# Hybrid attention layer on one core: a pacing ratio of its own for the latent projection between the chunked score tiles

## The chip, the core and the metric

The kernel runs on one core of a Trainium2 chip. A core has five engines with a queue each, which work in order: TensorE (PE in the profile; PEld is its loading of weights, which overlaps the matmuls), VectorE (DVE), ScalarE (ACT), GpSimd (POOL) and SyncE (SP), which here issues the transfers. The metric is the device time of one execution in microseconds (us). An engine's busy time is the sum of its instructions' durations.

## The reference

One layer of a streaming encoder on x of 1024 rows by 1024 columns, float32:

- an adaptive normalisation: six rows of shift, scale and gate from a conditioning vector times `w_ada`;
- one input projection of the normalised rows, whose columns are a query latent (256), a key and value latent (128), a rotary key (32), and queries, keys and values of eight chunked heads of 64;
- latent attention: the latents are normalised, projected up to eight heads (96 wide for queries and keys, 64 for values), normalised per head, rotated, and attend to all earlier chunks of 64 rows;
- chunked attention: eight heads, each chunk of 64 queries sees its own and the eight chunks before it, with a relative bias;
- an output projection with a gated residual, then a gated feed-forward part with a causal convolution of width 3, and a second gated residual.

```
q = rmsnorm(q_lat) @ w_q_up          # latent heads
kv = rmsnorm(kv_lat) @ w_kv_up
...
o_mla = mla_attention(q, k, v)       # 8 heads, chunk-causal
o_ca = chunk_attention(cq, ck, cv, rel_bias)   # 8 heads, band of 9 chunks
x = x + g_a * (concat(o_mla, o_ca) @ w_out)
```

## The kernel before

**Stages.** After a start in which the rows are normalised and transposed into `hT`, one long attention stage runs (in the profile some 540 us), then the output projection, the feed-forward part and the down projection. Matrix products are made with three matmuls each, since every operand is kept as a high and a low half (`gemm3`, lines 150 to 157).

**Score tiles.** The attention stage is a list of units: sixteen for the chunked heads, written here as chunked unit (p, g, o) with the pair of heads p, the half of the query rows g and the head o of the pair, then sixteen for the latent heads. Each unit has four tiles of 128 queries, so that tile 7 of unit (3, 1, 1) is the last chunked one. A tile (`scores`, lines 774 to 866) makes its scores on TensorE (`sc` for the chunked heads, `sm` for the latent ones), takes the minimum on DVE, the exponential on ACT, scales on POOL and DVE into two half-precision parts (`hlc`, `hlm`) and has a transposing transfer turn them (`PTc`, `PTm`). Three tiles later `values` (lines 868 to 906) multiplies the turned tiles of a pair with the values (`pvc`, `pvm`), and writes a finished half of a head to memory (`oc`, `om`, then `oT_d`).

**Fillers.** Between the tiles stand steps of the projections that are needed later, in a fixed order (lines 963 and 964): the remaining chunked projections, then "m", the latent projection (`f_m`, lines 502 to 536), "up0" and "up1", the two latent up projections (`f_up`, lines 628 to 691), and "oca", half of the output projection. "m" has 38 steps: for each of eight row tiles four steps of six matmuls into `mp`, after every fourth tile three steps that turn the latents into a page of `latT` (transposes into `lt_ps`). A row tile's matmuls are followed by its normalisation on ACT and POOL (`lat`). An up projection has 16 steps, two for each row tile, `qu` and `ku`; a tile's results go through ACT and POOL, and through eleven instructions of DVE, into `qn`, `kn` and `vt`. Before its first step it loads its weights `wq` and `wk` through two buffers that `f_m` also uses (`qtile`, line 141), splits them into halves on ACT and POOL, and makes a scale (`vspm`).

**Pace.** `pace` (lines 1005 to 1012) is called after the scores of every tile and after every `values`, with a written cost in nanoseconds of what was just issued. It adds that cost times a ratio to a debt and issues filler steps, which bring their own written cost, until the debt is paid. The ratio is `R_CA` = 1.9 for a chunked unit and `R_MLA` = 0.5 for a latent one. `need` (lines 996 to 1001) issues at one go whatever a unit must have and isn't issued yet: the first latent unit needs all of "up0", the second (the upper half of the same head) all of "up1". Every 1700 ns of written cost of most fillers, "m" among them, also issue a step of `f_ada` (lines 436 to 479), which loads and sums the remaining rows of the adaptive normalisation.

**What sets an engine's order.** The order in which the program issues is not yet the order of a queue. The framework orders each engine's queue while the kernel is built: of the instructions that are ready it takes the one with the lowest position, which is the place in the program; a block under `high_priority(offset=n)` counts as if it stood n places earlier. Scores and their softmax stand 400 places earlier (`OFF_S`), the scaling and the transfer 200 (`OFF_P`), the values 200 (`OFF_V`); fillers, and the pages that a unit prepares, stand at their own place. A filler step must also stay behind the fifth-last block of scores or values issued before it (`gemm3_f`, `LAG`).

Of the kernel before, what the change touches and what calls it, by code (L numbers as in the profile page):

```python
# [43 lines left out]
MODE_C = "1111"  # L44
MODE_M = "1111"
PSCALE, VSCALE = 2.0 ** 15, 2.0 ** 14
R_CA, R_MLA = 1.9, 0.5


C_C, C_GA, C_GM, C_B, C_GQL, C_GKL = 0, 8, 16, 24, 72, 74  # L50
# [14 lines left out]
def layer_kernel(ctx, tc, I, out):  # L65
# [331 lines left out]
    def f_qk(p):  # L397
        with tc.issue_after(r_last):
            w, _ = weights(f"qk{p}")
        for h in range(2):  # L400
            qns[p, h] = pgtile([P, 4, 256], F32, f"qn{p}_{h}")
        for t in range(0, NT, 2):
            pt = ps.tile([P, 512], F32, name=f"ipq{p}_{t}", tag="mm", bufs=2)
            yield from proj2(pt, t, w, 256)
            qk_norm(pt[:], f"{p}_{t}", qns[p, t // 4], t % 4)

    def f_v(pp):
        w, ssw = weights(f"v{pp}") if pp else (wv0, ssw0)
        for t in range(0, NT, 2):
            h, j = divmod(t, 4)  # L410
            if t == 0:
                for i in range(2):
                    vts[2 * pp + i] = apg.tile([P, NT, 2, 2, 64], F16, name=f"v{2 * pp + i}", tag="v16", bufs=3)
            pt = ps.tile([P, 512], F32, name=f"ipv{pp}_{t}", tag="mm", bufs=2)
            yield from proj2(pt, t, w, 256)
            if t == 0:
                vscale["c", pp] = pow2_scale(f"c{pp}", ssw[:], hb[:], ND, 2.0 * D)
                sc = vscale["c", pp][0]
            for i in range(2):
                vt = vts[2 * pp + i][:, t:t + 2]  # L420
                src = pt[:].rearrange("p (t q a b) -> p t q a b", t=2, q=2, a=2)[:, :, i]
                act.activation(vt[:, :, :, 0, :], src, AF.Copy, scale=sc)
                dve.scalar_tensor_tensor(vt[:, :, :, 1, :], src, sc, vt[:, :, :, 0, :], op0=MUL, op1=SUB)
# [282 lines left out]
    def f_oca():  # L706
        ws = [load_wo(4, n, "a", "p") for n in range(2)]
        for t in range(NT):
            lo = rtile(f"cl{t}", (P, 4, P), F32R)
            hi = rtile(f"ch{t}", (P, 4, P), F32R)  # L710
            sp.dma_start(f32(lo[:]), oT_d[4:8, :, t * P:(t + 1) * P].rearrange("k p t -> p k t"))
            hi_of("a", hi[:], f32(lo[:]))
            lo_of("p", lo[:], f32(lo[:]), hi[:])
            for n in range(2):
                pt = ps.tile([P, 512], F32, name=f"oc{t}_{n}", tag="mm", bufs=2)
                yield from gemm3_f(pt[:], [(hi[:, k], lo[:, k], ws[n][k][:, 0], ws[n][k][:, 1]) for k in range(4)])
                o = qtile(f"co{t}_{n}")
                act.activation(o[:], pt[:], AF.Copy)
                sp.dma_start(part_d[t][:, n * 512:(n + 1) * 512], o[:])
# [227 lines left out]
    def mla_unit(gr, hh, g):  # L947
        o = hh % 2

        def prep():  # L950
# [12 lines left out]
    fillers = [("v0", f_v(0)), ("qk1", f_qk(1)), ("qk2", f_qk(2)), ("v1", f_v(1)), ("qk3", f_qk(3)),  # L963
               ("m", f_m()), ("up0", f_up(0)), ("up1", f_up(1)), ("oca", f_oca())]
# [5 lines left out]
    def fill_step():  # L970
        while fillers:
            key, gen = fillers[0]
            try:
                c = next(gen)
            except StopIteration:
                done.add(key)
                fillers.pop(0)
                continue
            if key in ("qk1", "qk2", "v1", "qk3"):
                nstep[0] += 1  # L980
                if nstep[0] % 3 == 0:
                    one_ahead(fillers[1][0])
            if key == "qk1":
                if rope[0] is None:
                    rope[0] = rope_tables()
                with tc.issue_after(anchor["dve"]):
                    next(rope[0], None)
            if key not in ("v0", "up0", "up1", "oca"):
                nside[0] += c
                while nside[0] > 1700:  # L990
                    nside[0] -= 1700
                    next(side[0], None)
            return c
        return None
# [8 lines left out]
    debt = [0.0]  # L1003

    def pace(cost, ratio):
        debt[0] += cost * ratio
        while debt[0] > 0:
            c = fill_step()
            if c is None:
                debt[0] = 0.0  # L1010
                return
            debt[0] -= c
# [9 lines left out]
    for n in range(len(tiles) + DEPTH):  # L1022
        if n < len(tiles):
            u, i = tiles[n]
            if i % 4 == 0 and u not in ready:
                need(u.need)
                u.prep()
            if i % 4 == 2 and n + 2 < len(tiles):
                v = tiles[n + 2][0]
                if all(k in done for k in v.need):  # L1030
                    ready.append(v)
                    v.prep()
            pace(u.scores(i), R_CA if u.band else R_MLA)
        if n >= DEPTH:
            u, i = tiles[n - DEPTH]
            if i % 4 == 1:
                need(u.needv)
            if i % 2:
                pace(u.values(i), R_CA if u.band else R_MLA)
# [609 lines left out]
```

## Time and profile before

| what | us |
|---|---|
| median of three runs (1331.05 to 1333.88) | 1333.68 |
| the profiled execution, as timed | 1334.5 |
| its span from first to last instruction | 1332.7 |
| TensorE busy / its loading of weights | 1212.8 / 997.1 |
| DVE busy | 1088.7 |
| ACT busy | 622.3 |
| POOL busy | 572.3 |
| first and last matmul of the latent projection start at | 264.1 / 335.9 |
| last chunked score matmul starts at | 325.6 |
| first matmul of the first up projection starts at | 348.0 |
| first latent score matmul starts at | 374.7 |
| last latent score matmul starts at | 595.3 |

Rows of a view of groups give line, engine, operation and names, then minimum, median and longest duration in ns, or the busy time and the mean. A row of the timeline gives the start, the time that a merged run of equal instructions took, and, in brackets, for how long the engine had been idle before it and what ended that. A row of the view by windows gives, for a stretch of the span, its length and then busy time and count of PE, PEld, DVE, ACT and POOL, the granted TensorE clock as a share of full speed, and what the DMA engines did. A busy time of TensorE counts overlapping matmuls once, so that distances between starts tell more of its pace than single durations do.

### The profile page before, as it was taken

How to read it: one execution, taken by the hardware profiler on the slowest of the kernel's cores; microseconds unless marked ns; L12 is line 12 of the kernel's file. 1: busy time of each engine (PE TensorE's matmuls, PEld its weight loads, DVE VectorE, ACT ScalarE, POOL GpSimd, SP SyncE). 2: the span in 40 equal slices, each digit the busy share in tenths (PEclk: the TensorE clock that was granted, in tenths of full speed). 3: DMA queues.
4: the chain of work that ended last, by engine and by line, in shares of the span. 5: the costliest groups of instructions: out<-in, count | busy, mean ns of one | idle time of the engine just before them, and what ended most of it. 6: DMA issues, size and time to landing. Idle time of an engine off the chain costs nothing.

```text
span 1332.7 us, 18710 instructions
## 1 busy us (share of the span) xinstructions
PE 1212.8 (91%) x6168; PEld 997.1 (75%) x6168; DVE 1088.7 (82%) x1928; ACT 622.3 (47%) x1132; POOL 572.3 (43%) x610
## 2 busy tenths in 40 slices
PE   3899999989667798888889999999999998999998
PEld 3888878868555576666677888888888886888886
DVE  6979898877589967894779888898889986687667
ACT  5454654445555545553366444444443444443331
POOL 5476773675675633354615445444444541000000
PEclk9899999989878798997999999999999998999999
DMA  8416768766123685879702333333333336943441
GB/s 321 144 55 156 164 143 197 150 151 138 35 72 70 119 172 122 152 164 326 275 16 79 106 124 111 122 116 108 113 106 132 111 119 221 393 151 114 132 159 63
DMA packets 223689, 190.57 MB, mean 143 GB/s; under 512 B 148708, under 2 KB 166884, under 8 KB 223592
## 3 DMA queue, kind: packets, MB, share of 16 engines
q1 hardware_dynamic: 223592, 189.38, 50.3%
q8 instruction: 48, 0.79, 0.3%
q14 instruction: 49, 0.40, 0.1%
HBM read 117.24 MB, written 37.49 MB: 116 GB/s over the span
## 4 chain that ended last, share of the span: by engine, by line
PE 48%; DVE 3%; DMA 2%; issue 1%; ACT 1%; POOL 0%; SPq 0%; POOLq 0%; DVEq 0%
PE p L1125 10%; PE p L1126 10%; PE p L1127 10%; PE dnA_P L1460 2%; PE dnA_P L1461 2%; PE dnA_P L1462 2%; PE dnB_P L1461 1%; PE dnB_P L1460 1%; PE dnB_P L1462 1%; PE dnA L1461 1%; PE dnA L1460 1%; PE dnA L1462 1%; PE dnB L1461 1%; PE dnB L1462 1%; PE dnB L1460 1%
## 5 line engine op out<-in xcount | busy, mean ns | idle before, releaser
L77 ACT ACTIVATE dnP<-dnr 128x1024 fp32r<-128x1024 f32 x73 | 77.4, 1064 | 117.5 <-PE dnA_P L1462 46.4
L1434 DVE TENSOR_TENSOR dnP<-dnr,dnP 128x1024 fp32r<-128x1024 f32 x72 | 87.9, 1224 | 52.7 <-ACT dnP L77 47.7
L73 POOL TENSOR_SCALAR hlm<-Pm,rim 128x512 f16<-128x512 f32 (+2 forms) x96 | 65.4, 691 | 77.5 <-DVE rim L832 32.0
L84 POOL TENSOR_TENSOR wf<-wu,wf 128x512 fp32r<-128x512 f32 x22 | 39.8, 1808 | 118.2 <-ACT wf L77 118.2
L1296 DVE SCALAR_TENSOR_TENSOR u<-c,cvp,u 128x1023 f32<-128x1023 f32 x44 | 58.6, 1372 | 27.8 <-ACT u L1295 27.8
L84 POOL TENSOR_TENSOR wb<-wu,wb 128x512 fp32r<-128x512 f32 x22 | 42.2, 1920 | 75.0 <-ACT wb L77 59.6
L73 POOL TENSOR_SCALAR hlc<-Pc,ric 128x640 f16<-128x640 f32 (+2 forms) x64 | 48.0, 753 | 54.5 <-DVE ric L832 25.8
L851 DVE SCALAR_TENSOR_TENSOR hlm<-Pm,rim,hlm 128x512 f16<-128x512 f32 (+2 forms) x96 | 65.9, 696 | 5.5 <-POOL hlm L73 5.2
L829 ACT ACTIVATE Pc<-sc,mc 128x640 f32<-128x640 f32 (+2 forms) x64 | 42.2, 660 | 55.2 <-DVE mc L818 26.1
L891 PE MATMUL pvm<-PTm,vt 128*128 128x256 f16 (+1 forms) x320 | 47.7, 302 | 22.1 <-DMA PTm<-hlm 14.2
L829 ACT ACTIVATE Pm<-sm,mm 128x128 f32<-128x128 f32 (+3 forms) x64 | 47.1, 738 | 37.7 <-DVE mm L822 21.2
L1295 ACT ACTIVATE u<-c,cvp 128x1024 f32<-128x1024 f32 x44 | 52.4, 1238 | 26.0 <-DVE c L1394 18.0
L1297 DVE SCALAR_TENSOR_TENSOR u<-c,cvp,u 128x1022 f32<-128x1022 f32 x44 | 61.7, 1442 | 0.0
L891 PEld LDWEIGHTS <-vt 128*128 128x128 f16 x320 | 33.1, 111 | 37.0 <-issue 21.6
L77 ACT ACTIVATE wc<-ws 128x512 fp32r<-128x512 f32 x21 | 13.3, 632 | 91.9 <-DVE ws L1144 86.1
L154 PE MATMUL ipq<-wq_s,hT 128*128 128x256 f32 x192 | 55.7, 290 | 0.0
L156 PE MATMUL ipq<-wq_s,hT 128*128 128x256 f32 x192 | 55.4, 288 | 0.0
L155 PE MATMUL ipq<-wq_s,hT 128*128 128x256 f32 x192 | 55.1, 287 | 0.0
L851 DVE SCALAR_TENSOR_TENSOR hlc<-Pc,ric,hlc 128x640 f16<-128x640 f32 (+2 forms) x64 | 49.2, 774 | 6.8 <-POOL hlc L73 6.7
L1461 PE MATMUL dnA_P<-dnP 128*128 128x512 f32 x132 | 51.3, 389 | 0.0
L1462 PE MATMUL dnA_P<-dnP 128*128 128x512 f32 x132 | 51.3, 389 | 0.0
L1460 PE MATMUL dnA_P<-dnP 128*128 128x512 f32 x132 | 51.2, 389 | 0.0
(442 smaller groups left out, 4413.7 us busy)
## 6 DMA issues: line engine op xcount, KB each, us to landing
wu<-w_up SPq DMA_DIRECT2D x44, 512.0 KB, 3.5
dnr<-g_d SPq DMA_DIRECT2D x73, 256.0 KB, 2.8
aw<-w_ada SPq DMA_DIRECT2D x48, 256.0 KB, 3.4
g_d<-u SPq DMA_DIRECT2D x22, 512.0 KB, 3.0
dnr<-w_down SPq DMA_DIRECT2D x44, 256.0 KB, 5.4
adaw<-w_ada_a SPq DMA_DIRECT2D x16, 512.0 KB, 6.0
x<-x SPq DMA_DIRECT2D x16, 512.0 KB, 9.8
g_d<-gs SPq DMA_DIRECT2D x22, 256.0 KB, 2.8
```

The costliest lines, as they stand in the source:

```text
L73: pool.tensor_scalar(o, i, s, 1.0, op0=MUL, op1=MUL)
L77: act.activation(o, i, AF.Copy)
L84: (pool if eng == "p" else dve).tensor_tensor(o, i, f32(hi), op=SUB)
L829: act.activation(pr[:, :n], sv, AF.Exp, bias=m[:], scale=-1.0, accum_out=rsum[:, 0:1])
L851: dve.scalar_tensor_tensor(hl[:, w:2 * w], pp, ri[:], hl[:, :w], op0=MUL, op1=SUB)
L1125: pe.matmul(pt, sh, pg[:, 0], start=(k == 0 and not add), stop=False, skip_group_check=skip)
L1126: pe.matmul(pt, sh, pg[:, 1], start=False, stop=False, skip_group_check=skip)
L1127: last = pe.matmul(pt, sl, pg[:, 0], start=False, stop=(k == 3), skip_group_check=skip)
L1434: r = f(*a, **k)
L1460: pe.matmul(pt, sh, w[:, 0, 0], start=start, stop=False, skip_group_check=add)
L1461: pe.matmul(pt, sh, w[:, 1, 0], start=False, stop=False, skip_group_check=add)
L1462: pe.matmul(pt, sl, w[:, 0, 0], start=False, stop=stop, skip_group_check=add)
```

## The change

While the filler in front of the list is "m", the latent projection, `pace` replaces the ratio that it was given by `R_M` = 3.2. Nothing else is edited: no instruction is added or removed, and the values computed are the same. What changes is after which tile the steps of "m", of all fillers behind it, and of `f_ada`, are issued.

```
-R_CA, R_MLA = 1.9, 0.5
+R_CA, R_M, R_MLA = 1.9, 3.2, 0.5
...
     def pace(cost, ratio):
+        if fillers and fillers[0][0] == "m":
+            ratio = R_M
         debt[0] += cost * ratio
         while debt[0] > 0:
             c = fill_step()
```

More of the change, by code (lines that the diff above doesn't have):

```diff
@@ L46 @@
 PSCALE, VSCALE = 2.0 ** 15, 2.0 ** 14
-R_CA, R_MLA = 1.9, 0.5
+R_CA, R_M, R_MLA = 1.9, 3.2, 0.5
 C_C, C_GA, C_GM, C_B, C_GQL, C_GKL = 0, 8, 16, 24, 72, 74
@@ L1005, in pace @@
     def pace(cost, ratio):
+        if fillers and fillers[0][0] == "m":
+            ratio = R_M
         debt[0] += cost * ratio
```

## The prediction, made before the changed kernel had run

> **What bounds the kernel now.** I read the page first, then a view by windows around the place where the change acts (chunked heads end, latent heads begin), then the timelines of the engines there.
>
> ```profile
> span 1332.7 us, 18710 instructions
> ...
> PE 1212.8 (91%) x6168; PEld 997.1 (75%) x6168; DVE 1088.7 (82%) x1928; ACT 622.3 (47%) x1132; POOL 572.3 (43%) x610
> ```
>
> Over the whole span no engine is full, so the bound has to be found for each stretch:
>
> ```profile
> 298.00:312.00 14.00, 14.00 (x79) 12.72 (x78) 11.68 (x31) 6.99 (x23) 11.20 (x24) 1.00 0.83 188
> 312.00:326.00 14.00, 13.34 (x85) 10.38 (x83) 10.58 (x34) 5.93 (x13) 3.08 (x4) 1.00 0.61 122
> 326.00:336.00 10.00, 9.72 (x53) 9.43 (x53) 5.62 (x12) 5.93 (x25) 8.98 (x21) 1.00 0.41 80
> 336.00:348.00 12.00, 5.87 (x40) 4.41 (x39) 2.32 (x4) 5.67 (x16) 8.30 (x22) 0.70 0.38 94
> 348.00:375.00 27.00, 19.81 (x83) 14.62 (x83) 22.02 (x75) 16.52 (x39) 12.94 (x14) 0.94 0.03 8
> 375.00:460.00 85.00, 60.74 (x272) 45.91 (x272) 77.03 (x232) 46.82 (x112) 54.72 (x58) 0.78 0.41 89
> ```
>
> The reader is to see three stages. Up to 336 TensorE has no gap worth naming (14.00 of 14, 13.34 of 14, 9.72 of 10): the chunked heads and the latent projection are bound by it. From 348 DVE sets the pace (22.02 of 27, then 77.03 of 85). Between them lies a hole of 12 us in which TensorE is busy for 5.87 and DVE for 2.32, and the clock falls to 0.70. The order around the hole stands in TensorE's timeline and in the windows of `mp` alone:
>
> ```profile
> 320.63 1.16 PE L891 MATMUL pvc<-PTc,v 128*128 128x256 f16 x11
> ...
> 323.83 1.27 PE L891 MATMUL pvc<-PTc,v 128*128 128x256 f16 x12 [0.24 <-DMA PTc<-hlc]
> 324.91 0.59 PE L797 MATMUL sc<-k,qh 128*128 128x128 f32 x2
> 325.43 0.60 PE L797 MATMUL sc<-k,ql 64*128 64x128 f32 x2
> ```
>
> ```profile
> 312.00:326.00 14.00, 5.04 (x24) 4.35 (x24) 0.00 (x0) 1.00 0.61 122
> 326.00:336.00 10.00, 9.10 (x48) 8.91 (x48) 1.45 (x3) 1.00 0.41 80
> ```
>
> ```profile
> 335.86 0.35 PE L156 MATMUL mp<-wm_h,hT 128*128 128x416 f32 x1
> ...
> 338.96 0.33 PE L530 MATMUL lt_ps<-ident,lat 128*128 128x128 f32 x1 [1.43 <-POOL lat L522]
> 339.42 1.27 PE L891 MATMUL pvc<-PTc,v 128*128 128x256 f16 x12
> 342.12 0.47 PE L530 MATMUL lt_ps<-ident,lat 128*128 128x128 f32 x1 [1.43 <-POOL lat L522]
> 344.16 1.11 PE L530 MATMUL lt_ps<-ident,lat 128*128 128x128 f32 x4 [1.56 <-DVE latT L534]
> 346.84 1.11 PE L530 MATMUL lt_ps<-ident,lat 128*128 128x128 f32 x4 [1.57 <-DVE latT L534]
> 348.04 0.67 PE L154 MATMUL qu<-wq,latT 128*128 128x384 f32 x1
> ```
>
> The last chunked scores start at 324.91. Behind them 48 of the 192 matmuls of "m" (eight of its 32 matmul steps) run as one block, with no scores left to stand beside. After the block TensorE waits 1.43 + 1.43 + 1.56 + 1.57 = 6.0 us in four pieces, and "up0" starts at 348.04, 12.0 us after the last `mp` at about 336.05. That delay is a chain, which the other queues show:
>
> ```profile
> 337.39 1.12 SPq L637 DMA_DIRECT2D wqr<-w_qu  x2
> ...
> 343.40 0.33 SPq L643 DMA_DIRECT2D wkr<-w_kvu  x1
> ```
>
> ```profile
> 340.30 0.52 ACT L77 ACTIVATE wq<-wqr 128x384 fp32r<-128x384 f32 x1 [2.49 <-DMA wqr<-w_qu]
> ```
>
> ```profile
> 342.05 0.37 POOL L523 TENSOR_SCALAR lat<-lat,mr 128x128 f32<-128x128 f32 x1
> 342.38 1.95 POOL L84 TENSOR_TENSOR wq<-wqr,wq 128x384 fp32r<-128x384 f32 x2
> ```
>
> The loads of `wq` wait for the two buffers that the last row tiles of "m" use, their split waits on POOL behind the last `lat`, the load of `wk` (343.40) waits for the first split to free a buffer, and `vspm` and `qu` follow. It starts from the end of "m", wherever that lies.
>
> **The change part by part.** *Where the steps are issued* follows from the written costs. At 1.9 the 38 steps of "m" reach from tile 5 of unit (2,1,1) to the values issued just before the last chunked tile; "up0" gets four steps beside the tiles and twelve at one go in `need`. At 3.2 "m" ends with the values issued before tile 5 of (3,1,0), all 16 steps of "up0" follow by tile 6 of (3,1,1), `need` has none of it left, and the go of "up1" before the second latent unit falls from eight steps to four.
>
> *What the queues make of it* I count by places: a score tile some 15 instructions, a block of values 14, a step of "m" six and its share of the normalisation. Before, the last score tile, 400 places forward, outranks the later steps of "m", as the 48 matmuls behind it show. After, the last step of "m" stands about 30 places ahead of the last score tile even with its 400. Up to tile 6 of (3,1,0) the count gives the order that the trace already has, because until then the scores, not the steps, wait for their inputs. So only the last four score tiles move: 4, 5, 7 and 11 more steps of "m" ahead of them.
>
> *The end of "m".* What it overtakes no longer stands in front of it: the last score tile, 324.91 to 326.03 or 1.1 us, and two blocks of values, 1.16 + 1.27 us. Together 3.5 us, so "m" ends at about 332.6. Bounds: 0 if the order stays; if nothing but `mp` ran from 312 on, its 72 matmuls left there (24 + 48; 48 take 9.10 us, so 13.7) would end at 325.7, 10 us early, which the higher places of the earlier scores exclude. I take 3.5.
>
> *The start of "up0".* The overtaken 3.5 us fit into the 6.0 us of gaps in the hole. The chain keeps its 12.0 us, except that its splits on POOL now have the last tiles' work beside them. A split beside a busy DVE and one in the hole:
>
> ```profile
> L84 POOL TENSOR_TENSOR wm_l<-wm_r,wm_h 128x256 fp32r<-128x256 f32 x4 | 3.8, 950 | 3.7 <-ACT wm_h L77 3.6
> ```
>
> ```profile
> L84 POOL TENSOR_TENSOR wq<-wqr,wq 128x384 fp32r<-128x384 f32 x2 | 1.9, 994 | 0.0
> ```
>
> 950 ns for 256 columns against 994 for 384 (663 for 256) is 1.43 times as long. On two `wq` splits (1.95 us, 0.84 more) the price lies between 0 and 0.8; with about 6 us of moved tile work on DVE in 12 us, and a POOL scaling or two between, I take 0.7. "up0" starts 3.5 - 0.7 = 2.8 us earlier.
>
> The Trainium skill ("SBUF — State Buffer", "Who interferes with whom") speaks against the change here: VectorE and GpSimd share one port pair as an exclusive lock, and a two-input VectorE instruction keeps a reading GpSimd instruction out until it is done. By it a split that comes second waits whole scalings; the slower split above agrees with the direction.
>
> *The clock.* After the hole TensorE starts slowly:
>
> ```profile
> 351.23 0.34 PE L154 MATMUL qu<-wq,latT 128*128 128x384 f32 x1
> ...
> 353.55 0.34 PE L154 MATMUL qu<-wq,latT 128*128 128x384 f32 x1
> ```
>
> The first row tile's nine matmuls take 3.2 us (348.04 to 351.23), the second's 2.3 (to 353.55). A hole with 2.5 instead of 6.0 us of gaps may keep the clock up: 0 to 0.9 us, I take 0.5.
>
> *From 348 on* "up1" has five more steps ahead of the first latent unit's pages. In 348 to 375 DVE idles 18%, in 375 to 460, where latent tiles and "up1" mix, 9%. Mixed as well, 22.02 us of DVE would take 24.3: a gain of 2.7 at best. At worst a page waits for DVE with "up1" ahead of it, as here, 2.4 us:
>
> ```profile
> 383.42 0.45 PE L729 MATMUL mq_ps<-ident,qn 128*96 128x128 f32 x1 [2.37 <-DVE qn L500]
> ```
>
> Between +2.4 and -2.7 I take -0.7, since the work that moves up is what DVE lacks there.
>
> *`f_ada`.* Its calls and transfers stay, the remaining ones come up to a few tiles sooner, on SP ahead of some `PTc`:
>
> ```profile
> L460 DVE SCALAR_TENSOR_TENSOR aacc<-aw,cs,aacc 128x512 f32<-128x512 f32 x9 | 7.5, 830 | 0.1
> ```
>
> ```profile
> PE pvc L891 <- DMA PTc<-hlc: 1.9, 2, 1.6
> ```
>
> DVE has 5.7 us free in 298 to 326 and hides sums of 0.83 that slip by a tile; without that cover each would cost its 0.83 once. A late transfer has cost up to 1.6 us at one place. I take 0, with 1.6 as the upper end.
>
> **Sum:** -2.8 - 0.5 - 0.7 = -4.0 us. Against the profiled execution that is a span of 1328.7 and a time of 1330.5; its 1334.5 stands 0.8 over the median of 1333.68, so I predict 1329.7. What lies behind 605 us doesn't change in itself and is carried along.
>
> **Rivals.** *The tail of the chunked heads holds up "up0"* (slower). The last score tile now starts near 333 or 334. From there to the last values it takes 14.5 us before (324.91 to 339.42), some of it in POOL's queue:
>
> ```profile
> 334.88 1.09 DVE L851 SCALAR_TENSOR_TENSOR hlc<-Pc,ric,hlc 128x640 f16<-128x640 f32 x1 [3.95 <-POOL hlc L73]
> ```
>
> So the last `pvc` is due at 348 to 352 (3.95 us of waiting behind `lat` may come twice). If it still stands ahead of `qu` in TensorE's queue, as it does before by 8.6 us, "up0" waits for it plus 1.3 us and starts at 349.3 to 353.3. It decides from a last transfer that lands later than about 346.7. Price +1.3 to +5.3, middle 3.3: 1337.0. For it: the queue is in order and POOL is busy 8.30 of 12 in the hole. Against: by place `qu` comes before the last two blocks of values.
>
> *The order doesn't change.* If readiness, and not places, decides, the 48 matmuls stay behind the last score: 1333.7. For it: up to 312 the trace goes by readiness. Against: from 320 the steps of "m" are ready and yet let two blocks of values and the last tile pass.
>
> *The splits lose to DVE.* If each of the chain's three splits waits out one scaling like the 1.09 us above, they cost 3.3 instead of 0.7: the sum is -1.4, 1332.3. For it: the split of 950 ns. Against: 3.3 us of such scalings is all that the moved tiles have in the hole. The rule of the Trainium skill ("SBUF — State Buffer") cited above leads here.
>
> *The hole closes.* If the tail also keeps TensorE filled, all 6.0 us of gaps go, with the clock's 0.9 and the 2.7 of mixing: -9.6, 1324.1. For it: the moved work is of the right size. Against: the chain from the end of "m" is untouched.
>
> **How the numbers follow.** Forecast 0.40, tail 0.24, no change 0.16, splits 0.06, hole closed 0.14. About 0.2% or 2.7 us is what a measurement of this kernel tells from no change. The forecast's own range, from the bounds of the clock, the mixing and the transfers, is 1326 to 1333; three quarters of it lie over 2.7 us. Faster: 0.31 of the forecast's 0.40, the 0.14, and 0.02 of no change, 0.47. Slower: 0.20 of the tail's 0.24, 0.03 of no change (the queues after 460 are ordered anew as well) and 0.05 of the forecast by the upper ends of mixing and transfers: 0.28. The rest, 0.25, is the same. For 8 in 10 the range takes in the closed hole, a little beyond it, and the tail to its upper end: 1322 to 1339.
>
> **What would show it.** Right: no block of `mp` behind the last `sc`; `mp` ends near 332 or 333; `sc` ends after it; `qu` starts near 345; the windows before 312 as they are. Wrong: `qu` starts at 348 or later with a `pvc` just ahead of it that waited for `PTc` (tail); 40 or more `mp` behind the last `sc` (no change); a start of `qu` before 343 (hole closed). If the first up projection is earlier and the time is not, the gain went between 348 and 605, and the latent scores' first and last start tell where.

## The result and the profile after

The changed kernel took 1352.22 us (median of four runs, 1348.96 to 1354.44) against 1333.76 beside it: a ratio of 1.0137 with a 95% interval of 1.0109 to 1.0165. It is 18 us slower, outside the range that was given. The profiled execution has the span of the first line here; the second is the page's line of busy times.

```profile
span 1352.7 us, 18718 instructions
...
PE 1222.1 (90%) x6168; PEld 1004.3 (74%) x6168; DVE 1095.3 (81%) x1928; ACT 623.0 (46%) x1132; POOL 582.8 (43%) x610
```

The same instructions are done in 20 us more. The view by windows of the kernel after, for the stretches shown of before (length, then busy time and count of PE, PEld, DVE, ACT, POOL, then clock, DMA share, GB/s):

```profile
298.00:312.00 14.00, 14.00 (x78) 12.87 (x77) 7.15 (x15) 4.42 (x17) 11.19 (x24) 0.95 0.65 174
312.00:326.00 14.00, 11.30 (x69) 10.57 (x68) 3.34 (x6) 5.33 (x19) 3.09 (x13) 1.00 0.15 37
326.00:336.00 10.00, 8.07 (x47) 7.67 (x45) 1.88 (x3) 5.32 (x20) 8.12 (x24) 1.00 0.07 20
336.00:348.00 12.00, 10.56 (x32) 7.55 (x33) 9.57 (x27) 5.40 (x12) 7.43 (x11) 0.54 0.41 92
348.00:375.00 27.00, 20.15 (x97) 14.28 (x95) 23.86 (x80) 14.24 (x35) 13.74 (x15) 0.83 0.41 79
375.00:460.00 85.00, 57.56 (x281) 44.51 (x282) 78.05 (x228) 50.08 (x118) 55.57 (x54) 0.84 0.32 75
```

DVE's column tells the story. From 298 to 336 DVE did 27.9 us of work before; now it does 12.4. TensorE, full before, has 4.6 us of idle time there. The work turns up from 336 on, where the latent heads need DVE for themselves. What went missing in 298 to 336 are the last eight chunked score tiles, as TensorE's timeline of the kernel after shows:

```profile
301.76 0.47 PE L797 MATMUL sc<-k,qh 128*128 128x512 f32 x1
302.16 0.50 PE L797 MATMUL sc<-k,ql 64*128 64x512 f32 x1
307.85 0.38 PE L530 MATMUL lt_ps<-ident,lat 128*128 128x128 f32 x2
...
322.47 0.66 PE L530 MATMUL lt_ps<-ident,lat 128*128 128x128 f32 x4 [1.57 <-DVE latT L534]
327.92 0.60 PE L729 MATMUL q_ps<-ident,qn 128*128 128x128 f32 x4
333.06 0.57 PE L797 MATMUL sc<-k,qh 128*128 128x512 f32 x2
333.48 0.60 PE L729 MATMUL k_ps<-ident,qn 128*128 128x128 f32 x4
336.29 0.33 PE L797 MATMUL sc<-k,qh 128*128 128x128 f32 x1 [2.22 <-DVE k L762]
```

Between 302 and 333 there is no chunked score. The rows to look at are `q_ps` and `k_ps`: the transposes that make the query and key pages of the last two chunked units (pair 3, upper half). The same three kinds of rows in TensorE's timeline of before:

```profile
284.26 1.11 PE L729 MATMUL q_ps<-ident,qn 128*128 128x128 f32 x4
289.63 0.66 PE L729 MATMUL k_ps<-ident,qn 128*128 128x128 f32 x4
304.19 0.38 PE L530 MATMUL lt_ps<-ident,lat 128*128 128x128 f32 x2
```

Before, these pages were made at 284 and 290, and the latent pages (`lt_ps`) followed from 304 on. After, the three latent pages come first, and the chunked pages follow at 328 and 333. A score cannot start before its pages are there.

The reason is a buffer. `lt_ps` (line 528) and `q_ps`, `k_ps` (line 726) are tiles of one tag, "T", of which there is one buffer in PSUM. The account that e1 to e4 test is that a buffer is handed from tile to tile in the order in which the program asks for it. The pages of unit (3,1,0) are asked for at tile 2 of unit (3,0,1). By the written costs, at a ratio of 1.9 the latent pages come after that point, and at 3.2 the first half's three pages are issued ahead of it. After that `q_ps` has to wait for them, whatever its priority.

### The profile page after: what moved, and what is told of

It is laid out like the page before. It is cut to its first block, busy times and chain, and to the rows that moved or that the text cites. A ratio compares the mean times of both kernels' runs of the same rounds, so it can differ in the third digit from the quotient of the medians.

```text
span 1352.7 us, 18718 instructions
## 1 busy us (share of the span) xinstructions
PE 1222.1 (90%) x6168; PEld 1004.3 (74%) x6168; DVE 1095.3 (81%) x1928; ACT 623.0 (46%) x1132; POOL 582.8 (43%) x610
## 5 line engine op out<-in xcount | busy, mean ns | idle before, releaser
L73 POOL TENSOR_SCALAR hlm<-Pm,rim 128x512 f16<-128x512 f32 (+2 forms) x96 | 69.7, 735 | 92.4 <-DVE rim L832 39.8
L851 DVE SCALAR_TENSOR_TENSOR hlm<-Pm,rim,hlm 128x512 f16<-128x512 f32 (+2 forms) x96 | 68.9, 728 | 10.7 <-POOL hlm L73 10.3
L73 POOL TENSOR_SCALAR hlc<-Pc,ric 128x640 f16<-128x640 f32 (+2 forms) x64 | 52.3, 821 | 48.5 <-DVE ric L832 12.0
```

The costliest lines, as they stand in the source:

```text
L73: pool.tensor_scalar(o, i, s, 1.0, op0=MUL, op1=MUL)
L851: dve.scalar_tensor_tensor(hl[:, w:2 * w], pp, ri[:], hl[:, :w], op0=MUL, op1=SUB)
```

## The experiments

Each kernel is the one before or the one after with one or two edits. Starts are those of the first and last matmul of a tile in the trace of each; "latent scores" gives the first and last `sm`, and how far they lie apart. A whole row can be up to 5 us early or late, as the latent projection itself starts between 263.4 and 268.2. The ratio is against the kernel before run beside each, whose median lay between 1331.94 and 1336.10; rows are best compared by it. Each trace is of a single execution, up to 4 us off the median.

| kernel | median us | ratio, 95% interval | last `q_ps` | last `sc` | last `mp` | first `qu` | latent scores |
|---|---|---|---|---|---|---|---|
| before | 1333.68 | | 285.0 | 325.6 | 335.9 | 348.0 | 374.7 to 595.3: 220.6 |
| after | 1352.22 | 1.0137 (1.0109 to 1.0165) | 328.2 | 359.2 | 332.9 | 344.6 | 383.7 to 622.0: 238.3 |
| e1 | 1340.69 | 1.0057 (1.0040 to 1.0073) | 285.6 | 328.1 | 337.5 | 348.0 | 373.8 to 601.1: 227.3 |
| e2 | 1344.69 | 1.0086 (1.0058 to 1.0115) | 322.7 | 353.1 | 343.4 | 360.0 | 389.5 to 608.4: 218.9 |
| e3 | 1338.41 | 1.0039 (1.0015 to 1.0063) | 289.2 | 330.2 | 345.1 | 354.4 | 382.0 to 605.6: 223.6 |
| e4 | 1345.20 | 1.0090 (1.0061 to 1.0119) | 325.2 | 354.4 | 329.6 | 339.9 | 381.4 to 611.6: 230.2 |
| e5 | 1323.13 | 0.9921 (0.9901 to 0.9941) | 285.5 | 328.6 | 335.1 | 345.2 | 373.2 to 590.5: 217.3 |
| e6 | 1333.42 | 1.0000 (0.9982 to 1.0019) | 288.4 | 332.0 | 336.6 | 347.5 | 374.1 to 603.3: 229.2 |
| e7 | 1333.52 | 1.0003 (0.9987 to 1.0019) | 287.8 | 328.9 | 339.1 | 351.4 | 378.3 to 597.2: 218.9 |
| e8 | 1338.41 | 1.0047 (1.0028 to 1.0066) | 284.9 | 325.4 | 334.8 | 345.4 | 371.0 to 602.8: 231.8 |
| e9 | 1333.82 | 1.0015 (1.0000 to 1.0030) | 285.4 | 325.7 | 337.4 | 348.7 | 375.7 to 602.6: 226.9 |
| e10 | 1332.23 | 1.0002 (0.9988 to 1.0017) | 283.4 | 327.0 | 333.7 | 344.6 | 371.2 to 598.7: 227.5 |
| e11 | 1323.62 | 0.9941 (0.9926 to 0.9957) | 285.9 | 327.7 | 334.2 | 344.2 | 372.1 to 588.6: 216.5 |
| e12 | 1323.10 | 0.9906 (0.9868 to 0.9943) | 289.5 | 332.5 | 339.2 | 349.6 | 376.6 to 588.9: 212.3 |

### Whose turn it is in the transposing buffer: e1 to e4

**e1** asks for the pages earlier, five score tiles ahead of where the change does, and leaves the rest of the change as it is.

```
+            if u is units[12] and i == 1:
+                ready.append(units[14])
+                units[14].prep()
-            if i % 4 == 2 and n + 2 < len(tiles):
+            if i % 4 == 2 and n + 2 < len(tiles) and tiles[n + 2][0] not in ready:
```

> The changed kernel, but the pages of the last chunked half pair (units (3,1,0) and (3,1,1)) are prepared at tile 1 of unit (3,0,0), so before the first page step of the latent projection asks for the one transpose buffer T. Theory A (the one buffer T is handed out in program order; the denser steps put the latent pages ahead of the chunked pages, and the last eight chunked tiles wait for them): last q_ps near 285 instead of 328, last chunked score near 325 instead of 359, and the 20 us are gone: ratio to before 0.995 to 1.003. Theory B (the later issue of the up projections and of the output half is what costs, in the latent heads): q_ps moves back all the same, but the latent heads stay some 15 us longer: ratio 1.008 to 1.014.

**e2** goes the other way: the kernel before, without the denser steps, but with these pages asked for only when their unit begins.

```
-            if i % 4 == 2 and n + 2 < len(tiles):
+            if i % 4 == 2 and n + 2 < len(tiles) and tiles[n + 2][0] is not units[14]:
```

> The kernel before (ratio 1.9), but those pages are prepared only when their unit begins, which in program order is behind the three latent pages of the first half. Theory A: the slowdown without the change: last q_ps behind 310, last chunked score at 345 to 360, ratio 1.008 to 1.016. Theory B: chunked scores late, but the time within 5 us of before, since the fillers are issued as before.

**e3** is the change, with the latent pages in the tag of the projections' two PSUM buffers.

```
-name=f"lt_ps{h}_{b}", tag="T", bufs=TB)
+name=f"lt_ps{h}_{b}", tag="mm", bufs=2)
```

> The changed kernel, but the latent pages' transposes go into the two buffers of the projections (tag mm) instead of T; places are unchanged. Theory A: q_ps back near 285, last chunked score near 325 to 330, ratio 0.995 to 1.006. Theory C (the chunked pages lose by their place alone, behind more steps of the latent projection): q_ps stays near 328, ratio as the changed kernel's, 1.011 to 1.017.

**e4** is the change, with the page transposes raised 400 places, but still in the one buffer.

```
-        with tc.issue_after(first[0]):
+        with tc.issue_after(first[0]), tc.high_priority(offset=OFF_S):
             for j in range(4):
                 pe.transpose(pt[:rows
```

> The changed kernel, but the transposes of all pages stand 400 places earlier, like the scores; the buffer T stays the only one. Theory A: no help, q_ps of the last half pair stays near 328, ratio 1.009 to 1.019. Theory C: q_ps near 285, last chunked score near 325, ratio 0.995 to 1.005.

TensorE's timeline shows the order of the transposes in each. e1:

```profile
285.06 0.82 PE L729 MATMUL q_ps<-ident,qn 128*128 128x128 f32 x4
289.94 0.63 PE L729 MATMUL k_ps<-ident,qn 128*128 128x128 f32 x4 [0.17 <-DVE ql L756]
306.17 0.38 PE L530 MATMUL lt_ps<-ident,lat 128*128 128x128 f32 x2
```

e2:

```profile
303.77 0.38 PE L530 MATMUL lt_ps<-ident,lat 128*128 128x128 f32 x2
...
322.34 0.65 PE L729 MATMUL q_ps<-ident,qn 128*128 128x128 f32 x4
325.83 1.08 PE L729 MATMUL k_ps<-ident,qn 128*128 128x128 f32 x4 [0.75 <-DVE ql L756]
```

e3:

```profile
288.77 0.66 PE L729 MATMUL q_ps<-ident,qn 128*128 128x128 f32 x4
293.24 0.66 PE L729 MATMUL k_ps<-ident,qn 128*128 128x128 f32 x4
307.82 0.38 PE L530 MATMUL lt_ps<-ident,lat 128*128 128x128 f32 x2
```

e4:

```profile
302.17 0.38 PE L530 MATMUL lt_ps<-ident,lat 128*128 128x128 f32 x2
...
324.86 0.60 PE L729 MATMUL q_ps<-ident,qn 128*128 128x128 f32 x4
330.23 0.60 PE L729 MATMUL k_ps<-ident,qn 128*128 128x128 f32 x4
```

The order is undone by an earlier request (e1) and by another buffer (e3), and not by a higher priority (e4). It can be brought about without the change by a later request (e2). That is the signature of a buffer handed out in the order of the requests. e4 leaves the order as it is, and yet its ratio is 0.47 points below the change's; it raises the transposes of all pages, so that TensorE's queue differs from 80 us on, and where the time comes from was not followed. e2, which asks two tiles later than the change does, prices the order by itself at 0.86%, 11.5 us; e1 takes 0.80% of the change's 1.37% away, 10.7 us. What e1 leaves is 0.57%, 7.6 us, between its two expectations: neither account is the whole.

The last column says where in the traces each of the two lies. e2 loses ahead of the latent scores (first one 14.8 us later) and nothing between them (218.9 against 220.6 us). e1 loses nothing ahead of them (373.8 against 374.7) and 6.7 us between them. The change as it was has both: 9.0 us ahead, since its "up0" starts early at least, and 17.7 between. The two don't add up place by place. The part of the kernel behind the last latent score takes 6.7 us of that back (730.7 us from its start to the end, against 737.4); in e2 and e1 it takes back 4.2 and 3.2, so that of e1's 7.6 us its trace, of one of its fastest executions, shows only 2.6.

### What the density itself costs: e7

**e7** is e1, but with everything behind "m" issued where the kernel before issues it. A filler without work holds "up0" back, and the debt is set to the value that it had before.

```
-("m", f_m()), ("up0", f_up(0)),
+("m", f_m()), ("gap", iter([1e12])), ("up0", f_up(0)),
...
             if i % 2:
+                if u is units[14] and i == 7:
+                    debt[0] = -936.7
                 pace(u.values(i), R_CA if u.band else R_MLA)
```

> The change with early pages (e1), but the two steps of the first latent up projection, and all that follows it, are issued where the kernel before issues them: only the latent projection and the adaLN steps beside it are denser. Theory B (the 7 us that e1 still lost lie in the earlier issue of up0, up1 and oca): 1331 to 1336 us, ratio 0.998 to 1.002, first qu at 347 to 349. Rival (the density of the latent projection itself costs them, by work on VectorE and GpSimd that collides with the score tiles): 1338 to 1342 us.

1333.52 against 1332.97, ratio 1.0003: no difference. The denser steps of "m" and of `f_ada` by themselves neither cost nor gain, and the reason is plain: all five queues come out in the same order as before, instruction by instruction. (The first `qu`, at 351.4, lies outside what was expected, but everything in this trace from the first `mp` on is 3.3 us late.) So what e1 still loses comes from the earlier issue of "up0", "up1" and "oca".

### Why 48 matmuls stand behind the last score: e5

If issuing "m" more densely changes no queue, then something else than the pace held its last steps back before. Eight row tiles of latents go through a tag "R" with four buffers, and the four of the first half stay in use until all three latent pages of that half have been turned. **e5** is the kernel before with the last four row tiles in another tag, that of the loads of `f_ada`, the last of which is issued at 297.5 us before.

```
-raw = rtile(f"lat_{t}")
+raw = (rtile if t < 4 else atile)(f"lat_{t}")
```

> The kernel before, with one change: the last four latent row tiles (4 to 7) take buffers of tag A instead of tag R, so that the last two row tiles of the latent projection no longer wait until the three latent pages of the first half are transposed. In the queue before, 48 latent matmuls (mp) stand behind the last chunked score tile; here 26 do. Theory R (those 48 are held there by the four R buffers, not by the pacing): the last sc runs later than 325.6, the latent matmuls behind it take 6 us rather than about 10, and the hole on TensorE between the last mp and the first qu gets shorter: 1329 to 1333 us, ratio 0.996 to 0.999. Rival (the end of the chunked tail on VectorE and ScalarE sets when the last latent page can be transposed, and TensorE is not short there): the first qu stays at 348 or comes later, 1333 to 1338 us.

1323.13 us, ratio 0.9921: it beats both kernels, by more than was expected. The view by windows of `mp` alone, in e5, split where its last chunked score ends (329):

```profile
300.00:326.00 26.00, 17.66 (x89) 15.99 (x88) 2.06 (x4) 1.00 0.49 100
326.00:329.00 3.00, 2.00 (x11) 1.66 (x9) 0.00 (x0) 1.00 0.42 84
329.00:348.00 19.00, 5.15 (x26) 4.79 (x26) 1.03 (x2) 0.86 0.53 110
```

26 `mp` stand behind the last score, where before there were 48, and from the start of the last `mp` to that of the first `qu` it takes 10.1 us instead of 12.1. So the place of 22 of those matmuls was set by the row buffers; what holds the other 26 is open. Of the 11.7 us by which the traced span is shorter, 4.8 are there by the last latent score and 6.8 by the start of the last matmul of the output projection (`op`, 654.9 against 661.7). That the other 4.9 come from the freed matmuls is not shown: from that start to the end it takes 671.0 us before and 669.4 in e7, whose queues are the same, and 666.1 in e5, but also 665.5 to 667.7 in the change, e1, e4, e6 and e8 to e12, five of which have the old row buffers, and 669.2 and 668.5 in e2 and e3.

### What is left, with the row buffers free: e6, e8 to e12

**e6** is e1 and e5 together: the change, with both buffers out of its way.

> The change, with the pages of the last chunked pair prepared five score tiles earlier (as in e1) and the last four latent row tiles in tag A (as in e5): neither the transposing buffer nor the row buffers stand in the way of the denser steps. Theory B1 (the density itself pays once both buffers are out of the way): 1326 to 1332 us, below e5 and below before. Theory B2 (what e1 still lost, some 7 us, comes from the first latent up projection being issued among the last eight chunked tiles, and that is still here): 1336 to 1342 us, about 5 to 7 above e5.

At 1333.42 us it stands 10 us above e5, so the rest of the change costs here too, and more than the 5 to 7 that were expected; it is lost between the latent scores (229.2 against 217.3 us). That the number itself lies between the two expectations comes from e5 being faster than thought.

**e8** is e1 with "up1" and "oca" held back until the latent tiles begin, and paced from there as before. "up0" stays early.

```
-("up0", f_up(0)), ("up1", f_up(1)),
+("up0", f_up(0)), ("gap", iter([1e12])), ("up1", f_up(1)),
...
+            if n == 64:
+                need(["up0", "gap"])
+                debt[0] = -227.8
             pace(u.scores(i), R_CA if u.band else R_MLA)
```

> The change with early pages (e1): the first latent up projection is issued among the last eight chunked tiles as the change does, but the second one and the output projection of the chunked heads are held until the mixing tiles begin and are paced from there as before. Theory B2 (up0's instructions between the last chunked tiles push those tiles' later halves behind latent work in the queues of GpSimd and ScalarE): 1338 to 1342 us, and the latent score tile 6 comes 4 to 5 us later than before, as in e1. Theory B3 (the earlier issue of up1 and oca collides with the mixing score tiles): 1332 to 1336 us.

1338.41 us, ratio 1.0047, as e1 within the intervals: by time, "up0" alone is enough for the loss. By place the expectation missed: latent score tile 6 is reduced by DVE at 409.6 us, 1.8 us later than before and not 4 to 5, and the loss grows to 8.6 us by the last tile (607.1 against 598.5).

The early instructions of "up0" also stand among the tiles whose leads are counted in places. **e9** is e1 with 300 places more lead for the last two chunked units.

```
+            more = 300 if u in units[14:16] else 0
-            with tc.high_priority(offset=OFF_S):
+            with tc.high_priority(offset=OFF_S + more):
...
-            with tc.high_priority(offset=OFF_P):
+            with tc.high_priority(offset=OFF_P + more):
...
-            with tc.high_priority(offset=OFF_V):
+            with tc.high_priority(offset=OFF_V + (300 if u in units[14:16] else 0)):
```

> The change with early pages (e1), and for the last eight chunked score tiles (units 14 and 15) every lead in places is 300 larger: scores 700 for 400, probabilities 500 for 200, values 500 for 200. The first latent up projection is still issued among them. Theory P (the some 7 us that e1 and e8 lost come from places: the instructions of up0, issued between these tiles, use up the fixed leads, so that halves of their probabilities queue behind latent work): the lead is given back and the time comes to 1331 to 1336 us, with the latent score tile 6 within 2 us of the kernel before. Rival (the early issue of up0 costs by itself, by its weight splits or its loads): 1338 to 1341 us, as e1 and e8.

The time comes to 1333.82 us (interval 1.0000 to 1.0030, apart from that of e1), and tile 6 to 408.8 us against 407.9 before and 412.5 in e1, both as expected. But by tile 63 the trace is as late as e1's (606.9 and 604.0): between the latent scores the leads give nothing back for good, and what the whole kernel gained shows only behind them (728.3 us from the last latent score to the end, against 734.2). So the places account for a delay of some 4 us at the start of the latent tiles; that they are the cause of the whole 7 us is not shown.

**e10** puts e5, e1 and e9 together, and **e11** is e5 with the larger leads but without the change.

> The change with all three obstacles out of the way: early pages, the last four latent row tiles in tag A, and the larger leads of e9. Theory P: e6 lost some 10 us against e5 by places alone, so this comes down to 1321 to 1328 us. Rival (early up0 costs by itself): 1331 to 1335 us, as e6.

> The kernel before with the last four latent row tiles in tag A (e5) and the larger leads of e9, without the change. Under theory P up0 is not issued among these tiles here, so that the leads were long enough: 1321 to 1327 us, as e5 within 3 us. If it is faster than e5 by more than 3 us, the leads were too short in the kernel before as well, and what e9 and e10 gain by them says nothing of the change.

e10 is a miss for the places: 1332.23 us, as e6, where 1321 to 1328 were expected. e11 is as e5. The two traces run together to tile 42 (DVE reduces it at 530.6 and 531.0 us; the expectation of e12 goes by the write just ahead of that, at 529.7 and 529.5) and then part: 601.5 and 590.5 at tile 63. **e12** therefore holds "up1" and "oca" back in e10, with the edit of e8.

> e10 (the change with early pages, free row buffers and the larger leads), and the second latent up projection and the output projection of the chunked heads held until the mixing tiles begin and paced from there as before, as in e8. e10 kept pace with e11 up to latent score tile 42 (529.7 against 529.5 us) and lost 8 us between the tiles 45 and 63, with 7.4 us instead of 2.9 of waits of TensorE for transposed probabilities (DMA PTm) there. Theory Q (the output projection comes one step earlier against the mixing tiles, and its loads and stores stand ahead of the transposes in SyncE's queue): 1321 to 1327 us, as e11. Rival (up0 issued early alone gives another built order of the mixing, whatever is done with up1 and oca): 1329 to 1333 us, as e10, with tile 63 again near 600 us.

1323.10 us, as e11, and the shortest latent stage of all, 212.3 us. With the row buffers free and the leads long enough, it is the earlier issue of "up1" and of the output projection of the chunked heads, among the latent tiles, that costs. TensorE's waits in 530 to 590 (what it waited for; us in total, times, longest) and the window of the same stretch, first in e10:

```profile
PE pvm L892 <- DMA PTm<-hlm: 7.4, 4, 2.1
PE sm L804 <- ACT Pm L830: 4.9, 4, 2.0
```

```profile
530.00:590.00 60.00, 48.83 (x258) 38.18 (x259) 45.48 (x116) 26.80 (x59) 23.85 (x31) 0.86 0.68 134
```

And in e12:

```profile
PE pvm L892 <- DMA PTm<-hlm: 3.0, 3, 1.4
PE sm L804 <- ACT Pm L830: 1.8, 4, 0.7
PE mk_ps L729 <- DVE mq_0l L738: 0.7, 1, 0.7
```

```profile
530.00:590.00 60.00, 53.53 (x315) 41.62 (x313) 53.09 (x139) 32.59 (x71) 30.97 (x39) 1.00 0.75 159
```

In e10 TensorE waits 4.4 us more for turned probabilities and 3.1 more for the exponentials of the tiles before, DVE does 7.6 us less in the same 60 us, and the clock is 0.86 instead of 1.00. One of the waits in SyncE's queue of e10 there (same columns) is of the kind that was expected, a store of the output projection that holds the transposes behind it:

```profile
SPq L719 <- ACT co L718: 1.6, 1, 1.6
```

The same wait is 0.4 us in e12, so that it isn't the whole of the 8.6 us by which e10 is slower than e11. That the early issue of these two fillers costs them is shown by e12; by which of their instructions is open. Open too is what holding back alone would do with free row buffers and the short leads, since no run has that: in e8, with the row buffers as they were, it did nothing, and the two edits don't simply add up.

In sum, e12 has all of the change's density and its early "up0", and takes the same time as e5, which has neither. The change as such has nothing to give here.

## Why the prediction was wrong

**The failed step** is "So only the last four score tiles move", which rests on "Up to tile 6 of (3,1,0) the count gives the order that the trace already has". Places were counted and buffers were not. The last eight score tiles moved behind the latent pages, because their query and key pages share a buffer with these, and the last `sc` went from 325.6 to 359.2. Priced alone (e2) this is 11.5 us of loss that the sum doesn't have, in place of its gain. The rest of the measured loss stands under "From 348 on" below.

**The 48 matmuls** were put down to rank ("the last score tile, 400 places forward, outranks the later steps of 'm'"). e7 issues them earlier and nothing moves; e5 frees the row buffers and 22 of them do. So rank was not what held those 22, and even with the pages in time the step from 335.9 to 332.6 for the end of "m" had no ground (337.5 in e1, with the same 48 behind the last score).

**Two numbers that look right** are not. "m" ended at 332.9 (332.6 predicted) and "up0" started at 344.6 (345.2 predicted), but by leaving eight score tiles behind instead of overtaking four. That these two came out near is luck. Of the marks that were to show the step right, four were met with them (no block of `mp` behind the last `sc`, the end of `mp`, `sc` ending after it, the start of `qu`); only the fifth, that the windows before 312 stay as they are, told the truth: DVE fell from 11.68 to 7.15 us in 298 to 312.

**The clock** was to gain 0.5 us from a filled hole. It was 0.54 in 336 to 348 and 0.83 in 348 to 375, against 0.70 and 0.94 before; from 375 to 460 it was 0.84 against 0.78.

**From 348 on** the term was -0.7 within +2.4 and -2.7, "since the work that moves up is what DVE lacks there". With the pages in time (e1) it is a loss of 6.7 us between the latent scores. The bounds looked at the first pages only. The early issue of "up0" is enough for the loss with the row buffers as they are (e8); with these free and longer leads it is that of "up1" and the output projection, which shows 150 us later (e10 against e12).

**`f_ada`** at 0 was right, but not by the cover of DVE that was counted on: its loads don't come sooner. The last is issued at 297.5 us before, 298.8 after and 300.8 in e7.

**The rivals.** None came as a whole. "The order doesn't change", at 0.16, comes nearest to what held the 48 matmuls: with the pages in time (e7) readiness decides, the order of every queue is that of before, and the time is 1333.52, where the rival said 1333.7. The tail of the chunked heads did run into "up0", as the slower rival had it, but not by holding `qu` up: `qu` started early and then shared DVE with eight score tiles, its last matmuls starting at 448.6 where before it was 437.2. The splits that lose to DVE cannot be told apart in this trace, since the chain's queue around them is another one.

## What to carry to other kernels

When a step is moved in the program, list the buffers that it asks for, and who else asks for them between its old place and its new one. Here a tag with a single buffer, handed on in the order of requests, fixed an order that 400 places of priority did not undo, and eight score tiles waited behind the later request. Before a block of work in the wrong place is put down to pace or rank, see what buffers its producer is waiting for: here another tag for four row tiles brought 10 us, some 7 of them by the end of the output projection, where the change of pace was hoped to give 4.

## What the runs showed of the hardware

In the kernel after TensorE stalls for 8.59 us at 391.7 for one rotated query tile, where the longest such wait before was 2.43:

```profile
400.27 0.45 PE L729 MATMUL mq_ps<-ident,qn 128*96 128x128 f32 x1 [8.59 <-DVE qn L500]
```

DVE's timeline there, the same small operation undisturbed and, 8 us later, beside GpSimd's splits, and GpSimd's own:

```profile
388.08 0.21 DVE L500 TENSOR_TENSOR qn<-uqr 128x64 f32<-128x64 f32 x1
...
396.29 1.17 DVE L499 TENSOR_TENSOR qn<-uqr 128x64 f32<-128x64 f32 x1
397.38 1.63 DVE L851 SCALAR_TENSOR_TENSOR hlm<-Pm,rim,hlm 128x384 f16<-128x384 f32 x1
398.93 1.28 DVE L500 TENSOR_TENSOR qn<-uqr 128x64 f32<-128x64 f32 x1
```

```profile
396.08 1.29 POOL L84 TENSOR_TENSOR wk<-wkr,wk 128x512 fp32r<-128x512 f32 x1
397.33 2.80 POOL L84 TENSOR_TENSOR wo<-wor,wo 128x512 fp32r<-128x512 f32 x2
```

A DVE operation with two inputs on 128x64 took 1.17 and 1.28 us instead of 0.21 while GpSimd split weights. The Trainium skill ("SBUF — State Buffer", "Who interferes with whom") says that a VectorE instruction with two inputs in SBUF contends with a GpSimd instruction that reads SBUF, that the ports which they share are an exclusive lock, and that the order of issue decides which of them waits. The trace agrees: both operations start while a split runs and end 0.1 us after one does (397.46 and 400.21 against 397.37 and 400.13). The prediction had weighed this rule for the splits that come second. Here it is DVE that is held, by about a microsecond for an instruction of a fifth of that. From the start of the first of these operations to the end of the second are 3.9 of the 8.59 us; the rest was not followed. The longest of these operations took 1.3 us before as well, so by themselves they are not what the change costs.
